# Four of layer 1's eight modulation groups run between the experts of layer 0 and the norm of layer 1

## The chip, the cores and the metric

The kernel runs on one core of a Trainium2 chip. The metric is the time of the whole program in microseconds (us), as the device counts it; the median of several runs is quoted. The engines are PE (TensorE, matrix products), DVE (VectorE), ACT (ScalarE), POOL (GpSimd) and SP (SyncE, which here only issues DMAs). Each engine takes its instructions in the order in which the compiled program lists them.

## The reference, cut to what matters

Two layers of one trunk run over 256 context tokens and 256 latent tokens, with 1024 channels.

```python
for i in range(DEPTH):                       # DEPTH = 2
    mod = silu_c @ w_mod[i] + b_mod[i]       # (6*D) for the latent tokens
    modc = silu_cc @ w_mod[i] + b_mod[i]     # and for the context
    sh1, sc1, g1, sh2, sc2, g2 = ...         # six slices of D channels each
    h = rmsnorm(x, norm1_g[i]) * (1.0 + sc1) + sh1
    mix, mixc = mixing_sublayer(h, hc, w_in[i], ...)     # S5, SSD, attention
    x = x + g1 * mix
    h2 = rmsnorm(x, norm2_g[i]) * (1.0 + sc2) + sh2
    x = x + g2 * expert_choice_ffn(h2, ...)              # 16 experts
return rmsnorm(x, final_norm_g)
```

The six slices (`sh1`, `sc1`, `g1`, `sh2`, `sc2`, `g2`) are the kinds 0 to 5 of the kernel's modulation. Kinds 0 and 1 are needed by the norm in front of the mixing; kinds 2 to 5 not before the mixing's end.

## The kernel before, in words

`mod_group(l, kind, h)` (L157) computes half of one kind for both token sets. It issues four loads of 512 KB of `w_mod` (`load_w`, L103, on SP's queue) into the tile `w`, and eight small products per load (L165, 32 columns by 128); we call one load with its eight products a unit. The trace lists each product twice, so that a unit has 16 records. After four units ACT copies the result out (L168), PE transposes it (L169) and DVE writes it as `mcol` (L179, L181). A group is thus four units, and four groups are 16.

Groups wait in the list `todo`. `fill(n)` adds n credits and issues a group for every four credits. `win(c0, tiles, evac)` (L543) is the input projection: for each pair of 128-column tiles it takes two loads of `w_in` of 512 KB, calls `fill` unless `c0` is 0, and multiplies with `mm3`. Each such load goes raw into the same tile `w`; ACT rounds it to `wh` (L110), DVE or POOL subtracts to `wl` (L113), and PE multiplies with both (L122 and L125). The tile `w` has three buffers (`NW`), taken in turn by everything that loads into it: w_in, w_mod, and in the expert stage pieces of w_e_up and w_e_down. A load can be issued when the third load before it has been consumed.

At the start of layer 1's mixing two things follow on the experts' last `combine` (L1366 to L1370): the norm (`rs_tok`, L509 to L515) writes `xna` and `xnb`, and `xsave` puts the residual aside in DRAM (L517). Then `norm_rows` transposes them (L244, 8 row blocks), ACT scales and shifts them into `hrow` (L247), and DVE and POOL split them into `hh` and `hl`. `win(0, ...)` multiplies these with the first four w_in loads, and the small time-step projection (L747) follows. The later projections (`win(1024)` and `win(1536)` with a convolution behind them on DVE, then `win(512)`, `win(2576)`, `win(2064)`) run while DVE, POOL, ACT and PE also carry the S5 blocks (L610 to L723) and the SSD scan (L834 to L899).

The text of the kernel does not fix the order of an engine's instructions alone. The framework's scheduler lists them by its own timeline, so that instructions written later can stand earlier; SP's loads of one tile keep their order.

Of the kernel before, what the change touches and what calls it, by code (L numbers as in the profile page):

```python
# [34 lines left out]
DEPTH, D, T, N = 2, 1024, 512, 256  # L35
# [26 lines left out]
def r(ap):  # L62
    return ap.bitcast(F32R)
# [3 lines left out]
def tile_trunk(ctx: ExitStack, tc: tile.TileContext, a, out, dbg=None, stop=None):  # L67
# [14 lines left out]
    def bank(tag="ps"):  # L82
        return psm.tile([128, 512], F32, name="bk_" + tag, tag=tag, bufs={"mm": 3, "ps": 4, "s5": 1}[tag])
# [58 lines left out]
    todo = []  # L142
# [42 lines left out]
    def fill(n=1):  # L185
        credit[0] += n
        while todo and credit[0] >= 4:
            credit[0] -= 4
            mod_group(*todo.pop(0))
        if not todo:  # L190
            credit[0] = 0
# [49 lines left out]
    def transposed(xn, tts, k, sc, sh, pool, tag, bufs, btag="ps"):  # L241
        ps = bank(btag)
        for tt in tts:
            PE.transpose(ps[:, tt * 128:tt * 128 + 128], xn[tt][:, k * 128:k * 128 + 128], ident)  # L244
        h = pool.tile([128, 512], F32, name="hrow", tag=tag, bufs=bufs)
        for st in sorted({tt // 2 for tt in tts}):
            S.activation(h[:, st * 256:st * 256 + 256], ps[:, st * 256:st * 256 + 256], AF.Identity,  # L247
                         bias=sh[:, k, st:st + 1], scale=sc[:, k, st:st + 1])
        return h
# [213 lines left out]
    def mixing(l, mods):  # L463
        full = l == 0
# [56 lines left out]
        def norm_rows(ks):  # L521
            for k in ks:
                if full:
                    for kind in range(2):
                        mod_unit(0, kind, k, mw[k][kind])
                h = transposed(xn, [0, 1, 2, 3], k, mods["sc1"], mods["sh1"], bp, "t2", T2,
                               ("mm" if k % 2 else "s5") if full else "ps")
                V.tensor_copy(r(hh[:, k, :]), h)
                (G if k % 2 and not full else V).tensor_tensor(r(hl[:, k, :]), h, hh[:, k, :], op=OP.subtract)

        def hv(k, t0, t1):
            return r(hh[:, k, t0:t1]), r(hl[:, k, t0:t1])

        def wcols(wh, wl):
            return tuple(lambda m, k, v=v: v[:, k, m * 128:m * 128 + 128] for v in (wh, wl))
# [22 lines left out]
        if full:  # L558
            ub = [bank() for _ in range(4)]
            for kh in range(2):  # L560
                norm_rows(range(4 * kh, 4 * kh + 4))
                wu = []
                for i in range(0, 4, 2):
                    wu.append(load_w(a["w_in"][l], 4 * kh, 4, 128 * i, 256))
                if kh == 0:
                    for k in range(5, 8):
                        mod_load(k)
                for i in range(0, 4, 2):
                    wh, wl = wu[i // 2]
                    mm3(ub[i:i + 2], wcols(wh, wl), [lambda m, k=k: hv(4 * kh + k, 0, 512) for k in range(4)], kh == 0, kh == 1)  # L570
            for m in range(4):
                ev_u(m, ub[m])
        else:
            norm_rows(range(8))
            win(0, [0] * 4, ev_u)
        dump("hh%d" % l, hh)
        todo.extend((l, kind, h) for kind in range(2, 6) for h in range(2))
        if l + 1 < DEPTH:
            todo.extend((l + 1, kind, h) for kind in range(2) for h in range(2))
        sp = s5_params(l, slab) if full else X["sp"]  # L580
        c_lo = 0 if full else 32
        nl = 64 - c_lo
# [241 lines left out]
        for d in range(2):  # L824
# [4 lines left out]
            for ix, c in enumerate(seq):  # L829
# [17 lines left out]
                if need:  # L847
# [7 lines left out]
                    for g in range(2):  # L855
                        Rf = []
                        for p_ in range(2):
                            R = bp.tile([128, 4, 128], F32, name="R", tag="R", bufs=RB)
                            for q in range(4):
                                h = d * 8 + 4 * g + q  # L860
# [16 lines left out]
                        for q in range(4):  # L877
                            h = 4 * g + q
# [685 lines left out]
```

## Time and profile before

| | |
|---|---|
| runs | 2170.76, 2180.32, 2176.95 us; median 2176.95 |
| profiled execution | span 2175.6 us from the first to the last instruction; its time outside the span is not listed |
| PE, DVE, ACT, POOL busy | 86%, 48%, 26%, 27% |
| mean granted TensorE clock | 0.933 of full |
| stages | mixing of layer 0 to about 660 us, experts of layer 0 to 1214, mixing of layer 1 to about 1660, experts of layer 1 to the end |

A stage is read by its own rows: how long each engine was busy in it, the granted clock (PEclk, 1.00 is 2.4 GHz and 0.50 is 1.2 GHz) and what the DMA engines moved. A busy PE in such a row counts the tail of a pipelined product, so that a stretch of spaced products looks fuller than it is.

### The profile page before, as it was taken

The numbers are of one execution on the slowest core, as the hardware profiler recorded it, in microseconds if no ns is written. First come the engines' busy times: TensorE is split into PE (matmuls) and PEld (weight loads), VectorE is DVE, ScalarE is ACT, GpSimd is POOL, SyncE is SP. The second block draws the span as 40 slices with busy tenths as digits, with TensorE's granted clock in tenths as the row PEclk, the third lists the DMA queues.
The fourth block names the chain that finished last, engine by engine and source line by source line (L and its number), as shares of the span: only waits on it lengthen the run. The fifth ranks groups of instructions, "written<-read, shape, count | busy, mean of one in ns | idle before, by whom it ended". The sixth has DMA issues, their size and how long they took to land. (4 is left out here: it accounts for less than half of the span.)

```text
span 2175.6 us, 29618 instructions
## 1 busy us (share of the span) xinstructions
PE 1879.4 (86%) x11292; PEld 1127.1 (52%) x11292; DVE 1040.2 (48%) x2234; ACT 554.9 (26%) x1200; POOL 589.0 (27%) x644
## 2 busy tenths in 40 slices
PE   6899999999999997986897898989998997776675
PEld 4577777788787432322332576778897322111111
DVE  6888786663256227121123469788656222212122
ACT  4335644442343100000000433535443100000000
POOL 1645476542242002000003235486533000000000
PEclk9999989999998998998898998989998899999798
DMA  9464333336345998999999355343477899999997
GB/s 268 156 183 127 114 90 107 99 104 220 90 155 203 410 349 351 409 408 409 404 409 351 107 185 172 107 129 86 125 244 271 348 409 409 409 409 409 409 409 274
DMA packets 265310, 561.72 MB, mean 258 GB/s; under 512 B 44048, under 2 KB 132560, under 8 KB 264912
## 3 DMA queue, kind: packets, MB, share of 16 engines
q1 hardware_dynamic: 232864, 541.83, 68.0%
q10 hardware_dynamic: 32304, 18.00, 3.0%
q8 instruction: 89, 1.46, 0.3%
q14 instruction: 53, 0.43, 0.1%
HBM read 552.00 MB, written 7.77 MB: 257 GB/s over the span
## 5 line engine op out<-in xcount | busy, mean ns | idle before, releaser
L122 PE MATMUL bk_mm<-hh,wh 128*128 128x512 f32 (+1 forms) x704 | 254.2, 375 | 12.5 <-ACT xp L800 6.7
L122 PE MATMUL bk_mm<-hl,wh 128*128 128x512 f32 (+1 forms) x704 | 247.6, 365 | 0.0
L113 POOL TENSOR_TENSOR wl<-w,wh 128x1024 fp32r<-128x1024 f32 x64 | 157.0, 2452 | 223.5 <-ACT wh L110 171.1
L110 ACT ACTIVATE wh<-w 128x1024 fp32r<-128x1024 f32 x140 | 147.9, 1058 | 215.9 <-PE bk_mm L122 106.6
L125 PE MATMUL bk_mm<-hh,wl 128*128 128x512 f32 (+1 forms) x704 | 163.0, 361 | 1.5 <-POOL wl L113 1.5
L122 PEld LDWEIGHTS bk_mm<-hh,wh 128*128 128x128 f32 x704 | 139.6, 199 | 36.1 <-ACT xp L800 8.2
L122 PEld LDWEIGHTS bk_mm<-hl,wh 128*128 128x128 f32 x704 | 139.6, 199 | 17.7 <-issue 1.4
L113 DVE TENSOR_TENSOR wl<-w,wh 128x1024 fp32r<-128x1024 f32 x76 | 99.8, 1315 | 72.6 <-ACT wh L110 32.4
L125 PEld LDWEIGHTS bk_mm<-hh,wl 128*128 128x128 f32 x704 | 119.6, 195 | 20.0 <-POOL wl L113 1.7
L1389 PE MATMUL bk_mm<-rb,xeT 128*64 128x512 f32 x512 | 122.1, 601 | 3.3 <-DMA rb<-w_e_up 2.0
L1419 PE MATMUL bk_mm<-xw,xeT 128*32 128x512 f32 x448 | 107.3, 628 | 16.5 <-DMA xw<-w_e_gate 11.4
L1424 DVE SCALAR_TENSOR_TENSOR hd<-fth,bk_mm 64x512 f32<-64x512 f32 x16 | 10.9, 681 | 208.4 <-ACT fth L1422 208.4
L1441 DVE SCALAR_TENSOR_TENSOR YE<-bk_mm,grow 32x512 f32<-32x512 f32 x64 | 44.0, 687 | 129.6 <-PE bk_mm L1436 115.8
L1422 ACT ACTIVATE fth<-bk_mm 64x512 f32<-64x512 f32 x16 | 9.4, 590 | 377.7 <-PE bk_mm L1419 377.7
L1389 PE MATMUL bk_mm<-xw,xeT 128*64 128x512 f32 x320 | 82.1, 613 | 13.5 <-DMA xw<-w_e_gate 13.5
L603 POOL MEMSET rb<- 128x256 f32 x2 | 1.2, 588 | 319.0 <-PE bk_mm L1389 305.0
L1393 DVE SCALAR_TENSOR_TENSOR fth<-fth,bk_mm 128x512 f32<-128x512 f32 x16 | 11.0, 687 | 157.3 <-ACT fth L1392 157.3
L1389 PEld LDWEIGHTS bk_mm<-rb,xeT 128*64 128x64 f32 x512 | 40.1, 139 | 78.6 <-issue 69.8
L1409 DVE SCALAR_TENSOR_TENSOR YE<-bk_mm,grow 32x512 f32<-32x512 f32 x64 | 44.0, 687 | 73.3 <-PE bk_mm L1405 56.5
L1419 PE MATMUL bk_mm<-rb,xeT 128*32 128x512 f32 x304 | 68.0, 603 | 8.3 <-DMA rb<-w_e_up 6.1
L1366 PE MATMUL bk_ps<-YE,Gt 128*128 128x512 f32 x128 | 61.7, 612 | 11.9 <-DVE YE L1441 9.1
L1419 PEld LDWEIGHTS bk_mm<-xw,xeT 128*32 128x32 f32 x448 | 24.1, 114 | 88.7 <-issue 55.5
(560 smaller groups left out, 3883.5 us busy)
## 6 DMA issues: line engine op xcount, KB each, us to landing
xw<-w_e_gate SPq DMA_DIRECT2D x67, 1024.0 KB, 11.5
rb<-w_e_up SPq DMA_DIRECT2D x59, 1024.0 KB, 17.4
xw<-w_e_down SPq DMA_DIRECT2D x54, 1024.0 KB, 14.0
w<-w_in SPq DMA_DIRECT2D x92, 512.0 KB, 4.7
rb<-w_e_gate SPq DMA_DIRECT2D x43, 1024.0 KB, 16.6
w<-w_mod SPq DMA_DIRECT2D x80, 512.0 KB, 4.1
xw<-w_e_up SPq DMA_DIRECT2D x29, 1024.0 KB, 14.0
w<-w_e_down SPq DMA_DIRECT2D x46, 512.0 KB, 14.0
```

The costliest lines, as they stand in the source:

```text
L110: S.activation(r(hi), raw, AF.Copy)
L113: e.tensor_tensor(r(lo), raw, hi, op=OP.subtract)
L122: PE.matmul(ps, wh(m, k), xv, start=first and k == 0 and i == 0, stop=False)
L125: PE.matmul(ps, wl(m, k), xs[k](m)[0], start=False, stop=last and k == n - 1)
L1366: PE.matmul(ps, Gt[:, tt - tts[0], e // ne, :], YE[:, tt // 2 if full else 0, n, :], start=True, stop=True)
L1389: PE.matmul(ps[64 * n:64 * n + 64, :], xeT[:, k, e, :], w[:, n * 512:n * 512 + 512], start=k == 0, stop=k == 7)
L1393: V.scalar_tensor_tensor(th, th, 1.0, pg, op0=OP.add, op1=OP.mult)
L1409: V.scalar_tensor_tensor(YE[q0:q0 + 32, si, n, :], py[o:o + 32, :], 0.5, g2[o:o + 32, si, n * 512:n * 512 + 512], op0=OP.mult, op1=OP.mult)
L1419: PE.matmul(pg[o:o + 32, :], xeT[:, k, e, :], w[:, n * 512:n * 512 + 512], start=k == 0, stop=k == 7)
L1422: S.activation(th[:64], pg[:64], AF.Tanh, scale=0.5)
L1424: V.scalar_tensor_tensor(hd[64:128], th[:64], 1.0, pg[:64], op0=OP.add, op1=OP.mult)
L1441: V.scalar_tensor_tensor(YE[q0:q0 + 32, 0, n, :], py[o:o + 32, :], 0.5, g2[o:o + 32, 1, n * 512:n * 512 + 512], op0=OP.mult, op1=OP.mult)
```

## The change

Before, all eight groups of kinds 2 to 5 of layer 1 enter the list after `win(0)`, and `fill` draws them out among the projections. Now, for layer 1, they enter the list in front of the norm's transposes, and `fill(16)` issues four of them there: kinds 2 and 3. The other four (kinds 4 and 5) stay in the list and are drawn by the same calls as before. Layer 0 is untouched. Lines behind the edit move down by two.

```diff
         else:
+            todo.extend((l, kind, h) for kind in range(2, 6) for h in range(2))
+            fill(16)
             norm_rows(range(8))
             win(0, [0] * 4, ev_u)
         dump("hh%d" % l, hh)
-        todo.extend((l, kind, h) for kind in range(2, 6) for h in range(2))
-        if l + 1 < DEPTH:
-            todo.extend((l + 1, kind, h) for kind in range(2) for h in range(2))
+        if full:
+            todo.extend((0, kind, h) for kind in range(2, 6) for h in range(2))
+            todo.extend((1, kind, h) for kind in range(2) for h in range(2))
```

What the scheduler makes of it shows on SP first. The next rows are SP's loads before, from the last pieces of expert 15 (w_e_up, w_e_down) on.

```order
L1345 DMA w<-w_e_up 128x1024
L1345 DMA w<-w_e_down 128x2x512 x2
L1345 DMA wh<-w_e_down 128x2x512
L1345 DMA wl<-w_e_down 128x2x512
L106 DMA w<-w_in 128x4x256 x4
L742 DMA w<-w_in 128x8x16
L517 DMA xsave<-x 128x2x1024
L106 DMA w<-w_in 128x4x256
L106 DMA w<-w_mod 128x2x512 x4
L106 DMA w<-w_in 128x4x256 x2
```

These are the same loads on SP now.

```order
L1347 DMA wl<-w_e_down 128x2x512
L106 DMA w<-w_mod 128x2x512 x6
L517 DMA xsave<-x 128x2x1024
L106 DMA w<-w_mod 128x2x512 x10
L106 DMA w<-w_in 128x4x256 x4
L744 DMA w<-w_in 128x8x16
L106 DMA w<-w_in 128x4x256
L106 DMA w<-w_mod 128x2x512 x4
L106 DMA w<-w_in 128x4x256 x2
```

All 16 loads of the four groups now stand ahead of the four w_in loads of `win(0)`. Behind them two w_in and four w_mod loads alternate as before, until the last group; after it 13 w_in loads follow in a row.

On PE, these rows stood between expert 15's last products (L1405), the last `combine` (L1366) and `win(0)` before.

```order
L1405 MATMUL bk_mm<-wl,hT 64x512 x2
L1366 MATMUL bk_ps<-YE,Gt 128x512 x4
L244 MATMUL bk_ps<-kc,xna 128x128 x8
L244 MATMUL bk_ps<-kc,xnb 128x128 x8
L244 MATMUL bk_ps<-kc,xna 128x128 x2
L244 MATMUL bk_ps<-kc,xnb 128x128 x2
L122 MATMUL bk_mm<-hh,wh 128x512 x2
L244 MATMUL bk_ps<-kc,xna 128x128 x2
L244 MATMUL bk_ps<-kc,xnb 128x128 x2
L122 MATMUL bk_mm<-hl,wh 128x512 x2
```

On PE now, from the end of the last `combine` (L1368 here) to the first product of `win(0)`, these rows stand (units 8 and 9, pairs of L244 and an L169 are left out between the two pieces).

```order
L1368 MATMUL bk_ps<-YE,Gt 128x512 x4
L165 MATMUL bk_mm<-w,sil 32x128 x24
L169 MATMUL bk_mm<-kc,cpart 128x128
L165 MATMUL bk_mm<-w,sil 32x128 x8
L244 MATMUL bk_ps<-kc,xna 128x128 x8
L244 MATMUL bk_ps<-kc,xnb 128x128 x8
L165 MATMUL bk_mm<-w,sil 32x128 x8
```

```order
L165 MATMUL bk_mm<-w,sil 32x128 x24
L169 MATMUL bk_mm<-kc,cpart 128x128
L165 MATMUL bk_mm<-w,sil 32x128 x32
L169 MATMUL bk_mm<-kc,cpart 128x128
L122 MATMUL bk_mm<-hh,wh 128x512
```

Fourteen of the 16 units (x8 is one) stand behind the last `combine`, and no product of `win(0)` stands ahead of the last of them. The other two stand earlier: one in an S5 block beside expert 15, one behind expert 15's last products. From L747 on, PE's order is the same as before through 16 units of the later groups.

Then, in the SSD scan (L850 to L882), PE had these rows before.

```order
L715 MATMUL bk_s_9981<-rb_9574,rb_9573 128x32 x2
L165 MATMUL bk_mm<-w,sil 32x128 x2
L850 MATMUL bk_ps<-BC 128x128
L165 MATMUL bk_mm<-w,sil 32x128 x19
L880 MATMUL bk_ps<-wt,xdt 64x128
L882 MATMUL bk_ps<-e_9743,H 64x128
```

And now it has these there.

```order
L715 MATMUL bk_s_10165<-rb_9757,rb_9756 128x32
L717 MATMUL bk_s_10165<-rb_9758,rb_9757 128x32 x2
L852 MATMUL bk_ps<-BC 128x128
L882 MATMUL bk_ps<-wt,xdt 64x128
L884 MATMUL bk_ps<-e_9927,H 64x128
```

From the second half of the convolution to the attention's start, the 16 units that stood among the other work are gone, and projections of the later `win` calls stand earlier than they did.

## Rows read from the trace of the kernel before

**Rows 1.** The page: span, then busy share and instructions of PE.
```profile
span 2175.6 us, 29618 instructions
PE 1879.4 (86%) x11292; PEld 1127.1 (52%) x11292; DVE 1040.2 (48%) x2234; ACT 554.9 (26%) x1200; POOL 589.0 (27%) x644
```

**Rows 2.** Windows over the transition and layer 1's mixing: stretch, length, busy time per engine.
```profile
core 0: us, PE busy (x) PEld busy (x) DVE busy (x) ACT busy (x) POOL busy (x), PEclk, DMA share, GB/s
1185.00:1214.00 29.00, 26.24 (x80) 9.74 (x76) 17.43 (x25) 8.97 (x22) 10.78 (x11) 0.92 0.44 130
1214.00:1223.00 9.00, 4.25 (x19) 3.88 (x20) 5.60 (x32) 5.46 (x12) 0.14 (x2) 0.66 0.30 117
1223.00:1247.00 24.00, 24.00 (x115) 19.50 (x115) 9.31 (x12) 10.81 (x19) 10.06 (x6) 0.98 0.24 72
...
1271.00:1323.00 52.00, 46.13 (x349) 37.54 (x350) 47.31 (x77) 14.46 (x26) 23.24 (x30) 0.87 0.55 170
1323.00:1370.00 47.00, 37.34 (x359) 29.47 (x359) 40.28 (x83) 22.61 (x65) 22.12 (x28) 0.86 0.51 157
1370.00:1426.00 56.00, 55.36 (x520) 43.06 (x518) 41.13 (x89) 23.69 (x61) 32.51 (x37) 0.99 0.41 116
...
1450.00:1550.00 100.00, 92.33 (x750) 80.46 (x749) 79.12 (x190) 47.32 (x115) 61.62 (x65) 0.92 0.33 93
```

**Rows 3.** Timeline of PE there: start, length, instruction, [idle before <- releaser].
```profile
1207.53 1.88 PE L1405 MATMUL bk_mm<-wl,hT 128*64 128x512 f32 x4
1210.28 3.67 PE L1366 MATMUL bk_ps<-YE,Gt 128*128 128x512 f32 x8 [0.88 <-DVE YE L1409]
1218.28 1.94 PE L244 MATMUL bk_ps<-kc,xna 128*128 128x128 f32 x8 [4.33 <-DVE rs_u L216]
...
1223.17 1.00 PE L122 MATMUL bk_mm<-hh,wh 128*128 128x512 f32 x2
...
1224.23 0.38 PE L244 MATMUL bk_ps<-kc,xnb 128*128 128x128 f32 x2
...
1246.96 1.07 PE L747 MATMUL bk_mm<-hh,w 128*32 128x512 f32 x8
```

**Rows 4.** Timeline of SP: when runs of loads were issued, over how long.
```profile
1185.94 20.43 SPq L106 DMA_DIRECT2D w<-w_in  x4
...
1214.71 0.37 SPq L517 DMA_DIRECT2D xsave<-x  x1
1235.47 0.37 SPq L106 DMA_DIRECT2D w<-w_in  x1
1239.32 12.23 SPq L106 DMA_DIRECT2D w<-w_mod  x4
```

**Rows 5.** Timeline of ACT: the first two roundings of layer 1's w_in.
```profile
1190.84 1.06 ACT L110 ACTIVATE wh<-w 128x1024 fp32r<-128x1024 f32 x1 [1.39 <-DMA w<-w_in]
1207.73 1.06 ACT L110 ACTIVATE wh<-w 128x1024 fp32r<-128x1024 f32 x1 [4.13 <-PE bk_mm L1405]
```

**Rows 6.** The tile w_mod, layer 1's 32 loads: time from issue to landing.
```profile
DMA to landing us min/median/max: 3.6/4.2/5.7
```

**Rows 7.** Timeline of PE: two units in a row, and one that waited for its load.
```profile
1250.42 1.06 PE L165 MATMUL bk_mm<-w,sil 128*32 128x128 f32 x32
...
1330.29 0.65 PE L165 MATMUL bk_mm<-w,sil 128*32 128x128 f32 x16 [1.31 <-DMA w<-w_mod]
```

**Rows 8.** Windows: the four microseconds ahead of win(0).
```profile
1219.00:1223.10 4.10, 3.63 (x17) 3.23 (x16) 1.07 (x3) 2.55 (x5) 0.14 (x2) 0.50 0.00 0
```

**Rows 9.** Windows of line L165 alone (PE, PEld, clock, DMA): the last 16 units.
```profile
1323.00:1370.00 47.00, 7.33 (x128) 4.62 (x128) 0.86 0.51 157
1370.00:1426.00 56.00, 7.95 (x128) 3.92 (x128) 0.99 0.41 116
```

**Rows 10.** Timeline of PE: waits for DVE in the SSD scan and after it.
```profile
1344.11 1.22 PE L865 MATMUL bk_ps<-R,slr 128*128 128x512 f32 x2 [2.35 <-DVE H L899]
...
1435.58 0.39 PE L122 MATMUL bk_mm<-hh,wh 128*128 128x256 f32 x1 [1.22 <-DVE mcol L181]
```

## The prediction

> **What bounds the kernel now.** I read the page first: PE is the engine with the most work, 86% of the span of 2175.6 us [rows 1]. That is an average, so I went to the windows over the place that the change touches [rows 2]. The reader should see four different stretches there. Up to 1214 the experts of layer 0 end. From 1214 to 1223 nearly everything is idle: PE has 4.25 us of work in 9 us, the clock has dropped to 0.66 on average and the DMA engines move little. Here the norm of layer 1 is a chain: the timeline of PE shows the last `combine` ending at 1210.28 + 3.67 = 1213.95, a wait of 4.33 us for the norm's root on DVE, and the first product of `win(0)` at 1223.17 [rows 3]. From 1223 to 1247 PE is full (24.00 of 24.00 us) and DVE idles: `win(0)` takes 1246.96 - 1223.17 = 23.8 us, and its end releases everything that follows, the S5 blocks (through `us`) and the convolution. From 1271 to 1323 DVE is the fuller engine (47.31 of 52 us, 91%), and PE follows it. From 1323 on both are near full: PE 37.34 of 47 us, then 55.36 of 56 us, and 92.33 of the 100 us from 1450.
>
> The last view is SP's queue. Before, `win(0)` never waits for weights: its four loads were issued from 1185.94 on, as the buffers of `w` came free from expert 15 [rows 4], and ACT had rounded two of them by 1208.8, before the norm began [rows 5]. Those are the loads that now stand behind 16 others.
>
> **The change, part by part.** (a) *What 16 units cost at the transition, in PE time.* Two units in a row take 1.06 us, one alone 0.65 us [rows 7], so 16 take 8 to 10 us. PE has 4.75 idle microseconds from 1214 to 1223 [rows 2], so some of that is free. That is the smaller half.
>
> (b) *Their loads.* This sets the end. The tile `w` has three buffers: load n waits until unit n-3 has run on PE. A load lands 4.2 us after its issue (3.6 to 5.7) [rows 6], and a unit takes about 0.6 us, so three units go through in one round of 4.8 us, not 1.8. I follow the queue with the times of before. Load 1 takes the buffer that went to w_in at 1185.94; unit 1 runs beside an S5 block. Unit 2 follows on L1405, which ended at 1209.4 [rows 3]; loads 2 to 4 have landed by then, and load 5 is issued at about 1210. Units 3, 4 and 5 run behind the `combine`, at 1214.0 to 1215.7. Load 6, issued behind unit 3 at 1214.7, lands at 1218.9, and unit 6 runs to 1219.5. The first transposes (L244) stand behind it in PE's order and start at 1219.5, not at 1218.28: 1.2 us late. Load 7 stands behind `xsave` on SP, which waits for the residual until 1214.7 [rows 4]; it lands by about 1221 and is covered by the transposes. Unit 8 stands behind the transposes of the sixth row block, which ended at 1224.6 [rows 3] and now end near 1225.3; it ends at 1225.9. From there nothing covers the loads: unit 11 ends one round later, at 1230.7, unit 14 at 1235.5, and only then is the buffer free for the first w_in load. That lands at 1239.7, ACT takes 1.06 us to round it [rows 5], and `win(0)` starts at 1240.8 instead of 1223.2: **17.6 us late**. The 16th unit is through by about 1238.4 and does not hold it. Later w_in loads follow within a few microseconds and are hidden behind the first one's products.
>
> `win(0)` itself I leave at 23.8 us. It then has all rows of `hh` and `hl` ready, but it starts on a slow clock, as before (0.50 from 1219 to 1223.1) [rows 8]. So its end, and with it S5 and the convolution, comes about 17.5 us later. Bounds from the landing: three rounds and a load at the fastest landing, 3.6 us, give 4 x 0.6 = 2.4 us less, and with unit 8 not held by the transposes some 2 us less again, 13 us; at 5.7 us they give 6 us more, 23.5 us.
>
> The Trainium skill's page "DMA: Bandwidth & Descriptors", Rules for kernel authors, says to issue a DMA early, compute, and wait late, so that its fixed cost overlaps; it speaks against this order, which takes an early issue away from w_in. By the page's fit (2.0 us fixed, in its section Anatomy of one DMA) a 512 KB load would take 3.2 us, an estimate; the landing in the trace is a microsecond longer, and by the page the delay would be some 4 us smaller.
>
> (c) *xsave, ACT, DVE and POOL.* `xsave` keeps its place against the residual; its megabyte now shares the DMA with loads 6 to 8, inside the landing's spread. The four copies L168 and the `mcol` writes stand among idle stretches of ACT and DVE (5.46 and 5.60 of 9 us) [rows 2]. Nothing is charged. Without that cover they would cost under 1 us each.
>
> (d) *What the projections get back.* From L747 on, PE's order is unchanged through 16 units, up to about 1323 in the times of before. Over this stretch DVE leads (91%), and nothing is given back; the delay passes through. Behind it 16 units are gone. Their busy time is 7.33 + 7.95 = 15.3 us [rows 9], which counts the tails of short pieces; at 0.5 us a unit it is 8.2 us. Two waits go with them: 1.31 us for a load [rows 7] and 1.22 us of a projection for `mcol` [rows 10]. That gives 10.7 to 17.8 us at most. Not all of it comes back: in front of some pieces' successors PE waits for DVE anyway, 2.35 us at 1344.11 [rows 10], and from 1323 to 1370 PE has 9.7 idle microseconds as it is, with DVE at 86% [rows 2]. From 1370 to 1426 PE is full, and there 7.95 us of units are real time; afterwards the projections that were pulled forward shorten a PE that is over 90% full. I take **11.5 us**, with 5 and 17 as ends.
>
> *Sum.* +17.5 - 11.5 = +6 us. The experts of layer 1 start when the mixing ends and stream their weights from then, so the shift passes to the end. The profiled span of 2175.6 becomes 2181.6; the median of the runs is 1.35 us above that span, so the time is **2183 us**.
>
> **The rivals.** *Nothing is given back (slower).* The place is the SSD scan and S5 after 1323. Its point of decision is whether DVE (86%, then 73%) [rows 2] or its chain with ACT lets PE use the freed time. For it: from 1271 to 1370 DVE is fuller than PE, and the S5 blocks' start moves with `win(0)`. Against it: PE is full from 1370 to 1426. The return would be 5 us or less, and the time 2177 + 12.5 to 13 = 2190 us.
>
> *It evens out.* The delay is at its lower end, 13 us, and the return at 13 or more: 2177 us or a little less. For it: each round's landing near 3.6 us is within the rows.
>
> *The units gate the rest (faster).* Before, each pair of w_in loads stands behind four w_mod loads, and those wait for PE. With the later groups gone, 13 w_in loads follow each other, and the scan could close PE's 9.7 idle microseconds as well: a return of 17 + 8 = 25 us against 13, 2165 us. Against it: those idle times are waits for DVE.
>
> *The clock.* Before the first product of `win(0)` PE would run single units between waits from 1214 to 1241, and the clock stood at 0.50 after far less idleness [rows 8]. It is in the forecast as a start no faster than before; if it stayed low over the units too, each round would grow by half a microsecond, 1.5 us in all, inside the range. The Trainium skill, "TensorE: Matmul & The Clock Gate", HAM oscillation, describes short bursts of products between DMA waits that fall back to the low clock each time. The trace agrees for the 4.1 us in front of `win(0)`; no row here shows a longer run of bursts.
>
> That the change does not do what it says is excluded by the listed order: 16 units do stand at the transition.
>
> **How the numbers follow.** The forecast (a delay of about 17, most of the PE time given back) has 0.62. Nothing given back: 0.23. Evens out: 0.08. Faster: 0.07. About 0.5% (10.9 us) is what a measurement of this kernel can tell from no change. The forecast and the even case lie within it, 0.70; slower takes 0.23, faster 0.07. The range reaches from 2172 (even case and a little more) to 2192, which takes in most of the slower case.
>
> **What would show it.** In the profile after: the first product of `win(0)` near 1241 and L747 near 1264; one round of three units about 4.8 us apart between 1225 and 1238, PE waiting for DMA in front of them; a clock near 0.5 there; the conv stretch as long as before; and the stretch that answered to 1323 to 1426 shorter by some 8 us. The prediction is wrong if `win(0)` starts before 1235 (then the loads pipeline better than one round per landing), or if the stretch from L747 to the experts of layer 1 is not 5 us shorter than before.

## The result, and the profile after

The changed kernel takes 2196.65 us (median), the kernel before 2173.86 us in the same comparison: ratio 1.0097, 95% interval 1.0072 to 1.0122. It is slower by about 21 us; 2183 was forecast, with 2172 to 2192 as the range, and the measured time lies above it. The page of the profiled execution has a span of 2193.9 us, 18.3 more than before [rows 1], and PE with 3.0 us more busy time:

```profile
span 2193.9 us, 29598 instructions
PE 1882.4 (86%) x11292; PEld 1133.9 (52%) x11292; DVE 1039.8 (47%) x2234; ACT 556.2 (25%) x1200; POOL 589.1 (27%) x644
```

The transition, first on SP (start, length of the run of loads, instruction; before: [rows 4]):

```profile
1184.36 28.01 SPq L106 DMA_DIRECT2D w<-w_mod  x6
1212.47 0.42 SPq L517 DMA_DIRECT2D xsave<-x  x1
1212.98 21.07 SPq L106 DMA_DIRECT2D w<-w_mod  x10
1235.63 8.84 SPq L106 DMA_DIRECT2D w<-w_in  x4
```

The first w_in load left at 1235.63 instead of 1185.94. On PE the units stand as follows (timeline; before: [rows 3]):

```profile
1207.70 3.67 PE L1368 MATMUL bk_ps<-YE,Gt 128*128 128x512 f32 x8 [0.30 <-DVE YE L1411]
1211.30 1.52 PE L165 MATMUL bk_mm<-w,sil 128*32 128x128 f32 x48
...
1216.54 1.08 PE L165 MATMUL bk_mm<-w,sil 128*32 128x128 f32 x16 [2.99 <-DMA w<-w_mod]
...
1228.70 0.73 PE L165 MATMUL bk_mm<-w,sil 128*32 128x128 f32 x16 [2.04 <-DMA w<-w_mod]
1230.65 1.08 PE L165 MATMUL bk_mm<-w,sil 128*32 128x128 f32 x16 [1.22 <-DMA w<-w_mod]
...
1236.70 1.08 PE L165 MATMUL bk_mm<-w,sil 128*32 128x128 f32 x16 [1.14 <-DMA w<-w_mod]
1238.31 1.08 PE L165 MATMUL bk_mm<-w,sil 128*32 128x128 f32 x16 [0.53 <-DMA w<-w_mod]
...
1241.68 0.79 PE L122 MATMUL bk_mm<-hh,wh 128*128 128x512 f32 x1 [1.41 <-ACT wh L110]
...
1265.76 1.06 PE L749 MATMUL bk_mm<-hh,w 128*32 128x512 f32 x8
```

The reader sees single units, most of them with a wait for DMA in front, and `win(0)` at 1241.68, which waits for ACT to round the first w_in. The forecast had 1240.8 for that and about 1264 for the time-step projection (L749 here, L747 before); it came at 1265.76. The last six units start 9.61 us apart from first to last, 1.92 us each, so a round of three took 5.8 us, not 4.8.

So the delay was there. What was not there is the return. The next rows are windows (stretch, length, busy time and records of PE, PEld, DVE, ACT and POOL, granted clock, share of the DMA engines, GB/s) between landmarks of the mixing: from the time-step projection to the end of the BC convolution, to the end of the SSD scan, to the transpose of `dgr` (L973 before), to the last attention scores, to the end of attention, to the gated output of S5, to the first expert. First the kernel before, then the changed one.

```profile
1247.00:1346.60 99.60, 86.49 (x770) 67.56 (x770) 77.61 (x144) 30.62 (x67) 39.76 (x50) 0.91 0.59 184
1346.60:1415.30 68.70, 64.59 (x561) 50.31 (x561) 51.79 (x103) 35.85 (x98) 31.50 (x33) 0.92 0.40 116
1415.30:1459.90 44.60, 36.23 (x353) 31.89 (x349) 38.68 (x76) 17.80 (x37) 37.14 (x37) 0.96 0.48 138
1459.90:1536.90 77.00, 75.53 (x598) 64.54 (x598) 62.69 (x150) 38.28 (x92) 45.33 (x50) 0.94 0.33 93
1536.90:1563.00 26.10, 22.44 (x150) 21.98 (x150) 14.00 (x36) 9.08 (x19) 18.84 (x20) 0.80 0.34 78
...
sum 439.80, PE 395.71 PEld 338.67 DVE 318.36 ACT 179.24 POOL 216.99; mean PE 56.53 PEld 48.38 DVE 45.48 ACT 25.61 POOL 31.00
```

```profile
1265.80:1362.50 96.70, 82.84 (x718) 65.83 (x717) 77.42 (x144) 32.79 (x71) 39.27 (x50) 0.95 0.56 173
1362.50:1436.00 73.50, 64.12 (x522) 53.11 (x522) 60.77 (x120) 38.71 (x102) 40.22 (x41) 0.95 0.25 69
1436.00:1471.30 35.30, 23.53 (x175) 22.12 (x175) 29.80 (x59) 11.65 (x27) 30.06 (x32) 0.76 0.28 79
1471.30:1552.50 81.20, 80.01 (x589) 68.34 (x589) 60.84 (x144) 37.69 (x90) 42.59 (x49) 0.85 0.27 75
1552.50:1578.10 25.60, 23.44 (x145) 22.85 (x145) 15.54 (x35) 9.32 (x20) 17.12 (x20) 0.73 0.39 95
...
sum 438.40, PE 385.67 PEld 335.96 DVE 319.37 ACT 178.65 POOL 215.29; mean PE 55.10 PEld 47.99 DVE 45.62 ACT 25.52 POOL 30.76
```

PE is busy for 10.0 us less, with 16 units gone, and the whole is only 1.4 us shorter: PE's idle time grew from 44.1 to 52.7 us. Up to `dgr` 7.4 us had been won (212.9 to 205.5). The fourth window, with no unit in it before or after, then loses 4.2: about the same products (598 and 589 records) take 80.0 us instead of 75.5, at a granted clock of 0.85 instead of 0.94. In windows of 8 us from `dgr` on, the changed kernel has:

```profile
1464.00:1472.00 8.00, 2.75 (x35) 2.56 (x35) 6.92 (x26) 0.00 (x0) 3.23 (x4) 0.54 0.34 92
1472.00:1480.00 8.00, 6.81 (x18) 3.17 (x17) 8.00 (x22) 2.43 (x8) 4.93 (x9) 0.50 0.09 23
1480.00:1488.00 8.00, 8.00 (x52) 8.00 (x51) 3.80 (x10) 3.69 (x10) 4.10 (x7) 0.68 0.01 2
1488.00:1496.00 8.00, 8.00 (x34) 6.25 (x34) 6.26 (x13) 1.18 (x3) 5.40 (x7) 0.53 0.29 66
1496.00:1504.00 8.00, 8.00 (x60) 8.00 (x60) 5.45 (x12) 4.65 (x9) 0.17 (x1) 0.83 0.06 10
1504.00:1512.00 8.00, 8.00 (x72) 6.66 (x71) 4.26 (x8) 5.55 (x17) 3.96 (x2) 1.00 0.62 190
```

and the kernel before:

```profile
1452.60:1460.60 8.00, 4.01 (x62) 3.31 (x61) 7.65 (x24) 2.82 (x9) 4.63 (x3) 0.92 0.32 92
1460.60:1468.60 8.00, 7.18 (x23) 4.43 (x22) 5.76 (x16) 2.45 (x7) 5.68 (x7) 0.50 0.28 89
1468.60:1476.60 8.00, 8.00 (x64) 7.50 (x63) 6.89 (x21) 4.42 (x12) 4.94 (x11) 0.94 0.01 2
```

In both kernels the clock falls to 1.2 GHz (0.50) where PE has waited around `dgr`. Before, it is back within 16 us; in the changed kernel it rises once, falls again to 0.53 and is full only from 1504 on.

### The profile page after: what moved, and what is told of

Read it like the earlier page. It is cut to its first block, busy times and chain, and to the rows that moved or that the text cites. A ratio compares the mean times of both kernels' runs of the same rounds, so it can differ in the third digit from the quotient of the medians.

```text
span 2193.9 us, 29598 instructions
## 1 busy us (share of the span) xinstructions
PE 1882.4 (86%) x11292; PEld 1133.9 (52%) x11292; DVE 1039.8 (47%) x2234; ACT 556.2 (25%) x1200; POOL 589.1 (27%) x644
## 4 chain that ended last, share of the span: by engine, by line
PE 55%; DMA 23%; DVE 13%; POOL 3%; issue 2%; ACT 2%; SPq 1%; DVEq 0%; ACTq 0%; POOLq 0%
PE bk_mm L122 12%; PE bk_mm L1391 7%; PE bk_mm L125 6%; PE bk_mm L1421 4%; PE bk_mm L1407 3%; DMA wl<-w_e_up 3%; DMA wh<-w_e_up 3%; PE bk_ps L1285 3%; DMA rb<-w_e_up 2%; DMA xw<-w_e_gate 2%; DMA w<-w_e_up 2%; PE bk_mm L1438 2%; DMA w<-w_e_down 2%; DMA w<-w_e_gate 2%; PE bk_ps L1039 2%
## 5 line engine op out<-in xcount | busy, mean ns | idle before, releaser
L122 PEld LDWEIGHTS bk_mm<-hl,wh 128*128 128x128 f32 x704 | 140.9, 200 | 17.5 <-issue 1.0
L1426 DVE SCALAR_TENSOR_TENSOR hd<-fth,bk_mm 64x512 f32<-64x512 f32 x16 | 10.9, 681 | 208.9 <-ACT fth L1424 208.9
L165 PE MATMUL bk_mm<-w,sil 128*32 128x128 f32 x1280 | 60.1, 298 | 15.8 <-DMA w<-w_mod 13.8
```

What stands on the lines that cost most here:

```text
L122: PE.matmul(ps, wh(m, k), xv, start=first and k == 0 and i == 0, stop=False)
L165: PE.matmul(ps[32 * j:32 * j + 32, :128], sil[:, 2 * u + i, :], w[:, i, j * 128:j * 128 + 128], start=u == 0 and i == 0, stop=u == 3 and i ...
```

## The experiments

Each kernel's profile gives two lengths, beside the time of the whole. The **transition** runs from the start of the `combine`'s last product to the start of the time-step projection, 33.6 us before. The **rest** runs from there to the start of the last expert's last product, 914.0 us before. The table shows both as differences to the kernel before. Each is from one execution: the expert stage of layer 1 alone takes up to 2.5 us more than in the kernel before, and the `combine`, which both lengths leave out, comes between 6.9 us earlier and 6.5 us later than there (5.1 later in before_aheadlist, whose list is the kernel before's up to it). So the two lengths need not add up to the whole, and a difference of a few microseconds in one of them says little by itself. The changed kernel has +21.4 and -0.6; its `combine` came 2.6 us earlier, and that makes 18.2 of the 18.3 us.

| kernel | whole, ratio (95%) | transition | rest | order behind the time-step projection |
|---|---|---|---|---|
| after | 1.0097 (1.0072 to 1.0122) | +21.4 | -0.6 | its own |
| drop4 | 0.9961 (0.9942 to 0.9979) | -0.1 | -10.0 | its own |
| extra4 | 1.0151 (1.0128 to 1.0174) | +20.8 | +12.6 | its own |
| one | 1.0043 (1.0023 to 1.0063) | +3.3 | +7.6 | its own |
| two | 1.0009 (0.9997 to 1.0022) | +3.9 | -0.4 | its own |
| after_droplist | 1.0136 (1.0095 to 1.0177) | +34.2 | -9.6 | drop4's |
| drop_afterlist | 1.0039 (1.0018 to 1.0060) | +7.4 | -0.6 | after's |
| extra_beforelist | 1.0157 (1.0117 to 1.0197) | +33.8 | -5.9 | before's |
| before_extralist | 1.0102 (1.0067 to 1.0137) | +7.7 | +9.6 | extra4's |
| after_droplist2 | 1.0061 (1.0044 to 1.0079) | +21.5 | -7.9 | drop4's |
| before_extralist2 | 1.0071 (1.0049 to 1.0092) | +0.1 | +9.4 | extra4's |
| ahead | 1.0012 (0.9994 to 1.0031) | +16.5 | -20.3 | its own |
| ahead_droplist | 1.0051 (1.0031 to 1.0071) | +16.9 | -10.6 | drop4's |
| after_beforelist | 1.0104 (1.0084 to 1.0125) | +21.4 | -3.8 | before's, units left out |
| after_aheadlist | 1.0028 (1.0013 to 1.0043) | +21.7 | -14.6 | ahead's |
| before_aheadlist | 1.0100 (1.0080 to 1.0121) | +0.0 | +19.4 | ahead's, units put in |
| drop_beforelist | 1.0024 (1.0008 to 1.0039) | -0.1 | +0.3 | before's, units left out |
| behind_aheadlist | 1.0023 (1.0005 to 1.0041) | +17.1 | -20.5 | ahead's |
| behind | 1.0089 (1.0070 to 1.0108) | +17.1 | -1.0 | its own |

**The two halves apart, and smaller doses.** drop4 has only the return: the four groups are left out and constants stand in their place. extra4 has only the delay; one and two move one and two groups instead of four.

```diff
 # drop4, against the changed kernel
-            todo.extend((l, kind, h) for kind in range(2, 6) for h in range(2))
-            fill(16)
+            for kind in (2, 3):
+                mods[names[kind]] = const.tile([128, 8, 2], F32, name="mcol1_%d" % kind)
+                G.memset(mods[names[kind]], 0.5)
+            todo.extend((l, kind, h) for kind in range(4, 6) for h in range(2))
 # extra4, against the kernel before; mod_group writes duplicates with a tag into tiles of their own
+            for kind in (2, 3):
+                for h in range(2):
+                    mod_group(1, kind, h, "x")
             norm_rows(range(8))
 # one and two, against the changed kernel
-            fill(16)
+            fill(4)        # two: fill(8)
```

> The kernel before, with the first four of layer 1's modulation groups (kinds 2 and 3) left out altogether and their tiles filled with 0.5 instead; nothing is added at the transition. It measures alone what the projections give back when 16 units go. The theory of the prediction (PE time that is removed in the mixing mostly comes back, 11.5 us): about 2162 to 2165 us, 0.5% under the kernel before. The rival (the mixing of layer 1 is led by DVE and by chains, the units lie in PE's gaps): within 4 us of the kernel before.

> The kernel before, with all eight groups left among the projections and four more groups (the same products, into tiles that nobody reads) at the transition. It measures alone what the transition costs. The theory of the prediction (17.5 us there, and a return of 11.5 us that this kernel doesn't have): about 2191 us. The rival (20 us or more at the transition and no return worth the name): the same time as the changed kernel, 2194 to 2197 us, since taking the groups out of the projections is worth nothing.

> One group at the transition instead of four, seven among the projections. The first w_in load now waits for unit 2 alone, which ran at 1206.8, so win(0) should start near 1223 as in the kernel before. The theory of the prediction: no delay and a quarter of the return, 3 us under the kernel before. The rival: no delay and no return, the same time as before within 2 us.

> Two groups at the transition. The first w_in load waits for unit 6, which ran at 1217.6 in the changed kernel, so it lands near 1222 and win(0) starts near 1223 to 1225. Both theories: a delay of 0 to 3 us; with a return of 5 to 6 us (the prediction's) 2 to 6 us under the kernel before, without a return 0 to 3 us over it. If the cost went by units and not by rounds of landings behind unit 8, half of the 20 us would show: 10 us over.

As whole times, drop4 (2168.9 us) lies between its two forecasts, two (1.0009) agrees with no return, and extra4 (2208.8) and one (2187.0) are slower than either theory had them. The transitions bear out the rounds of landings: one and two pay 3.3 and 3.9 us for 4 and 8 units (none and 0 to 3 expected), the changed kernel 21.4 for 16, so the delay does not go by the number of units.

The rests do not add up. drop4 gives back 10.0 us in the rest, the changed kernel, with the same code behind the norm, 0.6. extra4 has exactly the kernel before's work in the rest and loses 12.6 there; one loses 7.6. So something moved the rest by some ten microseconds either way that is neither the work removed nor the delay. The lists of the built programs named a suspect: behind L747 drop4 and the changed kernel have the same instructions on every engine, but in another order, from the SSD scan on. That the edit at the transition shifts the timeline by which the scheduler lists is the likely reason; no run shows it apart. My forecast had looked at the order only up to the removed units.

**The order, crossed.** For these, the order that the scheduler gave one kernel was recorded and pinned in another, engine by engine, with edges that fix the place in the list and add no wait.

```diff
+    for i in tc.nc.cur_bb.bb.instructions[tc_mark[-1]:]:
+            lanes.setdefault(str(i.engine), []).append(i)
...
+        own = [lane[k] for k in tab[1:n + 1]]
+        for p, q in zip(own, own[1:]):
+            tc.add_manual_dep(q, p.name, dep, reason="list")
```

> The changed kernel; behind the norm of layer 1 each engine's instructions are pinned to the list that the kernel drop4 had there (the two have the same instructions behind the norm, so nothing is added or removed, only their order on each engine). In the profiles so far the stretch from the time-step projection to the end was 10.0 us shorter than the kernel before's in drop4 and 0.6 us shorter in the changed kernel. Theory that the list eats the return: the changed kernel loses about 9.4 us of its 2196.65, to some 2187, 1.0055 of the kernel before, with the transition as it was (about 21 us late against the last combine). Rival, that the later arrival itself eats it (loads, waits or the granted clock as that kernel meets them): no change, 2196 to 2197, about 1.010.

> The cross of the run above: drop4 (16 units fewer, none at the transition; four groups of layer 1 are not computed, so two modulation columns are constants) with the changed kernel's list behind the norm. Theory of the list: it loses about 9.4 us of what drop4 gained, 2168.9 to some 2178, about 1.002 of the kernel before. Rival, the later arrival: as drop4, about 2169, 0.996, since nothing arrives late here.

> extra4 (the kernel before plus four duplicate groups at the transition) with the kernel before's list behind the norm, where both have the same instructions. extra4 took 33 us more than the kernel before, of which its profile had 20.8 at the transition and 12.6 behind the time-step projection. Theory of the list: the 12.6 go, 2208.8 to some 2196, about 1.0095. Rival, the later arrival: they stay, about 2209, 1.015.

> The cross of the run above: the kernel before, no work added, with extra4's list behind the norm. Theory of the list: some 12.6 us slower than the kernel before, about 2188, 1.006. Rival, the later arrival: as the kernel before, 2175, 1.000.

As whole times all four came out slower than the theory of the order had them. For drop_afterlist its 1.002 lies inside the interval; the other three are misses, extra_beforelist close to its rival. The mark stood at the norm, and a foreign order of the norm and of the rounding of `win(0)`'s weights cost another 7 to 13 us in the transition. In the rest, however, three of them took what the order takes, not what the kernel takes: -9.6 where drop4 had -10.0, -0.6 where the changed kernel had -0.6, +9.6 where extra4 had +12.6. The fourth, extra_beforelist, has -5.9 where the kernel before's order gives 0 and extra4's own +12.6. The mark was therefore moved to the time-step projection.

> The changed kernel with drop4's list, pinned only from the time-step projection (L747 of the kernel before) on, so that the transition keeps the changed kernel's own list. In the four crossed runs before, whose pinning began at the norm, the projections of win(0) came later in all of them than their own lists had them (8.7 us later in the kernel before), but the stretch from the time-step projection to the last expert went with the list: drop4's list -10.0 in drop4 and -9.6 in the changed kernel, the changed kernel's list -0.6 in itself and -0.6 in drop4, extra4's list +12.6 in itself and +9.6 in the kernel before; the kernel before's list 0 in itself and -5.9 in extra4. Theory of the list: the changed kernel loses some 9 us of its 2196.65, to about 2187, 1.0055, with that stretch -9 to -10 and the transition +21 as it was. Rival, the later arrival: no change, 2196 to 2197, 1.010, the stretch at -0.6.

> The kernel before, nothing added or removed, with extra4's list from the time-step projection on; its own list up to there. Theory of the list: the transition as in the kernel before, the stretch behind it 9 to 13 us longer, together 2184 to 2188, 1.0045 to 1.006. Rival, that a late arrival eats the time: nothing arrives late here, so 2175, 1.000.

Both confirm it in the whole time. The changed kernel with drop4's order takes 2190.3 instead of 2196.65 (2187 expected); the kernel before, with nothing added and nothing late, takes 2191.8 instead of 2176.1 when it runs in extra4's order (2184 to 2188 expected). A late start cannot do that. Nor is it the pinning that costs: drop4's order takes -10.0 in drop4, where nothing is pinned, and -9.6, -7.9 and -10.6 where it is (after_droplist, after_droplist2, ahead_droplist). In the profile of before_extralist2 the windows from the end of the SSD scan to the last scores answer to rows three and four of the kernel before above:

```profile
1413.10:1470.80 57.70, 41.63 (x374) 36.64 (x375) 41.69 (x86) 19.25 (x43) 40.97 (x41) 0.80 0.42 121
1470.80:1554.10 83.30, 80.87 (x590) 69.75 (x589) 63.54 (x141) 38.98 (x91) 44.18 (x52) 0.85 0.26 75
```

The first of the two is 13.1 us longer, with 16.1 us of PE idle instead of 8.4, the second 6.3 us longer at the lower clock. Both carry nearly the records that they had (374 and 353, 590 and 598). What PE waits for longest there, between the end of the BC convolution and `dgr`, is a DMA of the S5 blocks, a wait that the kernel before does not have in that stretch (line, releaser, us, times, longest):

```profile
PE bk_s L833 <- DMA rb<-kd: 6.5, 2, 4.6
```

**What the units cost with the order held.** This is the term that I had to forecast, measured by itself: the kernel before's order, the 16 units left out of it.

> The changed kernel with the kernel before's list from the time-step projection on, the four groups that it no longer has there left out of the list and every other instruction in the kernel before's order: the units are taken from the projections without a new order. The prediction gave this return 11.5 us (5 to 17). If the units bounded the work there, the stretch from the time-step projection to the last expert is 10 to 11.5 us shorter than in the kernel before, 2196.65 less 10 gives 2186, 1.005. If they lay in time that PE waits through anyway, or kept TensorE's clock up there, the stretch is 0 to 4 us shorter, 2193 to 2197, 1.0085 to 1.010.

> drop4 (16 units fewer, none at the transition; two modulation columns are constants) with the kernel before's list from the time-step projection on, the missing units left out of it. In the run after_beforelist the stretch from the time-step projection to the last expert was 3.8 us shorter than in the kernel before, where drop4 with its own list had 10.0. If what taking the units away gives back is a matter of the list, it is 2 to 5 us shorter here too: 2175 less 4, some 2171, 0.998. If it is the early start that gives drop4 its 10 us, the stretch is 10 shorter here as well, 2165, 0.9955.

after_beforelist has -3.8 and 2196.5 us as a whole, inside the forecast for a small return. drop_beforelist has +0.3, and as a whole it is no faster than the kernel before (1.0024) although 16 units are gone; both of its forecasts were faster. These are the second and third window of drop_beforelist (the scan, and up to `dgr`):

```profile
1344.20:1411.80 67.60, 59.32 (x415) 47.38 (x417) 49.17 (x99) 35.30 (x96) 27.22 (x32) 0.82 0.21 56
1411.80:1458.90 47.10, 38.91 (x291) 36.41 (x286) 39.35 (x75) 17.75 (x36) 38.22 (x39) 0.78 0.31 89
```

With 208 records fewer than before (706 instead of 914) the two take 114.7 us instead of 113.3. PE idles 16.5 us there instead of 12.5, and what is left runs at 0.82 and 0.78 instead of 0.92 and 0.96. (after_beforelist has 112.1 us, at 0.83 and 0.85.) PE's longest waits in this stretch of drop_beforelist are the first of the next rows; under them stand three of the kernel before (line, releaser, us, times, longest):

```profile
PE bk_s L836 <- DVE rb L827: 4.8, 2, 3.1
PE bk_ps L972 <- DVE BC L938: 3.1, 1, 3.1
PE bk_ps L1002 <- DVE wt L991: 2.9, 1, 2.9
PE bk_s L769 <- ACT rb L764: 2.8, 1, 2.8
PE bk_ps L1095 <- DVE dgr L1094: 2.6, 1, 2.6
```

```profile
PE bk_s L648 <- ACT rb L643: 2.7, 1, 2.7
PE bk_ps L973 <- DVE dgr L972: 2.6, 1, 2.6
PE bk_ps L880 <- DVE wt L869: 0.8, 1, 0.8
```

ACT's `rb` and `dgr` were waited for before as well. The wait for `BC` and the one for DVE's `rb` (L836 here, L715 in the kernel before) are new, and the one for `wt` grew from 0.8 to 2.9 us: these are products in front of which units stood in the kernel before's list. S5 blocks and the scan hand results to and fro between DVE, ACT and PE. In this order the units filled gaps in that exchange, and the clock stood higher with them; taken away, they leave the gaps.

**The transition.** ahead gives the 16 loads buffers of their own, eight of them issued ahead of `xsave`, so that w_in keeps its three. behind also puts the products between the halves of `win(0)` and after it.

```diff
 # ahead, against the changed kernel: m8("mw") is a free tile of the layer's pool
+            for t_ in todo[:2]:
+                mod_ahead(*t_, m8)          # before xsave
...
+            fill(8)
+            for t_ in todo[:2]:
+                mod_ahead(*t_, m8)
+            fill(8)
-            fill(16)
 # behind, against ahead
+                with tc.issue_after(last):  # the last product of a half of win(0)
+                    fill(8)
```

> The changed kernel with the loads of its 16 units in buffers of their own (four free tiles of the layer's pool, two units each), the first eight issued ahead of the write of xsave, so that the three buffers of the projections keep the first w_in blocks, as in the kernel before. Theory that the rounds of landings through three buffers make the delay of win(0): from the last combine to the time-step projection 8 to 14 us longer than in the kernel before, in place of 21.4, since 10 us of products remain and 8 MB must land. Rival, that the products themselves make it (their clock, their place in PE's order): about 21 as before. What lies behind is the scheduler's new list and isn't known better than -10 to +10 by the lists seen so far: 2176 to 2196 in all, 1.0005 to 1.010.

> The kernel ahead with drop4's list from the time-step projection on. If both theories hold, the transition costs 8 to 14 us and the stretch behind gives back 10: 2171 to 2180, 0.998 to 1.002, a tie with the kernel before or a small gain. If the products make the delay, 2185, 1.005; if the list does nothing, as the kernel ahead.

> The changed kernel with the list of the kernel ahead from the time-step projection on (the same instructions behind it; in ahead that stretch was 20.3 us shorter than in the kernel before, in the changed kernel 0.6). Theory of the list alone: -20 here too, 2196.65 less 19.7 gives 2177, 1.0005, with the transition 21 us longer than in the kernel before as it was. Rival, that ahead's gain came with its buffers or its loads: the stretch at -0.6 to -10 as with the other lists, 2187 to 2197.

> The kernel before, all its work, with the list of the kernel ahead from the time-step projection on for the instructions that both have; the last four groups (and ScalarE's instructions up to the last of them) are left to the scheduler. ahead's stretch behind the time-step projection was 20.3 us shorter with 16 units fewer. If those 16 units cost their 10 us of products under this list, the stretch is about 10 us shorter than in the kernel before and the whole 2166, 0.995, faster than both kernels. If they lie in time that PE waits through, about 20 shorter, 2156, 0.991. If the list is worth nothing once the units stand in it, 2175, 1.000.

> The kernel ahead (16 units at the transition, their loads in buffers of their own), with the units no longer ahead of win(0) on TensorE: the first eight between its two halves, the other eight behind it, when their loads have landed; and ahead's list from the time-step projection on. The units then cost their products, about 10.4 us (16 of 0.65), in place of the 16.5 that ahead's transition took more than the kernel before's. With the list as in ahead and after_aheadlist (14.6 and 20.3 us shorter behind the time-step projection): 2175 + 10.4 less 14.6 to 20.3 is 2165 to 2171, 0.9955 to 0.998, faster than both kernels. If landings still hold TensorE there, 16 us stay and the whole ties, 2171 to 2177.

> The kernel above with the scheduler's own list behind the time-step projection. The transition as above, 10.4 us longer than in the kernel before; behind it the lists of these same instructions have given -0.6 to -20.3 so far: 2165 to 2185, 0.9955 to 1.0045.

The size of the transition was a miss in the four that move the loads: 16.5 to 17.1 us instead of 8 to 14 (ahead, ahead_droplist), or of 10.4 with the units behind `win(0)` (behind_aheadlist, behind). In behind_aheadlist the rows say why (POOL's timeline, PE's, then windows):

```profile
1231.00 0.10 POOL L944 MEMSET xp<- 128x4 f32 x1 [18.71 <-DMA xsave<-x]
...
1231.09 2.51 POOL L660 TENSOR_TENSOR hl<-hrow,hh 128x512 fp32r<-128x512 f32 x2
```

```profile
1232.41 0.80 PE L239 MATMUL bk_mm<-hl,wh 128*128 128x512 f32 x1 [5.97 <-POOL hl L660]
...
1244.56 3.25 PE L293 MATMUL bk_mm<-mw,sil 128*32 128x128 f32 x106
...
1260.05 3.05 PE L293 MATMUL bk_mm<-mw,sil 128*32 128x128 f32 x104
```

```profile
1230.00:1235.00 5.00, 2.59 (x6) 2.11 (x7) 1.48 (x3) 2.61 (x6) 2.60 (x4) 0.58 0.93 345
1235.00:1240.00 5.00, 5.00 (x18) 3.96 (x18) 2.37 (x3) 2.20 (x4) 3.27 (x3) 0.74 0.02 6
```

`win(0)` began on time here (1223.1), but then PE waited 5.97 us for POOL's half of `hl`: a clearing of `xp`, listed ahead of it on POOL, ran only when `xsave` had landed. `xsave` was issued at 1218.2 behind eight loads of 512 KB, with four more behind it from 1226.3 on, and landed at 1231.0. Of the 17.1 us the units take 8.1 (1244.56 to 1248.78 and 1260.05 to 1263.97), at full clock. The other 9 are this wait and what came after it: `win(0)` then runs at 0.58 and 0.74, where the kernel before had 0.98 over all of it [rows 2], and 9 less 5.97 leaves some 3 us for that, an estimate. In ahead the same clearing waited until 1231.38. Issuing `xsave` first was not run.

The order did the rest. ahead's own order is the best seen, 20.3 us shorter than the kernel before's rest, 20.5 in behind_aheadlist and 14.6 in the changed kernel, which falls from 2196.65 to 2180.4 by it (2177 expected). ahead in drop4's order falls back to drop4's rest, -10.6, and to 2188.2 as a whole (2171 to 2180 expected). ahead and behind differ only at the transition, by 0.6 us, and by 19 us in the rest: 2176.5 against 2191.5 us (for behind 2165 to 2185 was expected). It is not an order that carries over to other work: put into the kernel before, with the 16 units and ACT's instructions up to the last of them placed by the scheduler among it, it costs 19.4 us, where all three forecasts had a gain or a tie. That is 39.7 us over ahead's rest, 34 of them up to the end of the scan, where the units were put in. No version that does all the work beats the kernel before; ahead and two tie with it (1.0012, 0.9994 to 1.0031, and 1.0009, 0.9997 to 1.0022).

## Why the prediction was wrong, step by step

**(b), the delay: right in its mechanism, 3.9 us too small.** The first w_in load was issued at 1235.63; the prediction's queue had 1235.5, two rounds after unit 8. `win(0)` started 0.9 us later than forecast, the time-step projection within 2 us. That these times agree so well is in part luck: the `combine` came 2.6 us earlier in this execution. Against it the delay is 21.4 us, not 17.5, though inside the bounds of 13 to 23.5. The rounds were longer than forecast, 5.8 us, with landings of 3.6, 4.4 and 7.6 us (min, median, max) against [rows 6]. Issue early and wait late, the rule of the Trainium skill's page "DMA: Bandwidth & Descriptors" (Rules for kernel authors), holds here: the w_in loads that were issued 49.7 us later came too late for `win(0)`. The fit by which I had the delay some 4 us smaller stands on that page of the Trainium skill (Anatomy of one DMA) for DMAs that GpSimd issues, and these loads are on SP's queue; the measured landings decide.

**(a) and the clock: half right.** Fifteen units on PE from 1206.76 on sum to 12.4 us, over the 8 to 10 that I had, because seven of them ran at 1.08 us, where the granted clock was 0.67 (1222.0 to 1241.7), between its two levels of 1.2 and 2.4 GHz. I had priced this rival at 1.5 us in all; a round was 1.0 us longer than 4.8. The Trainium skill, "TensorE: Matmul & The Clock Gate" (HAM oscillation), describes such bursts between DMA waits that fall back to the low clock; this trace agrees, with those seven units. The 4.1 us of [rows 8], in which I had seen agreement, are transposes behind a wait for DVE and not such bursts.

**(c), nothing charged: right for this kernel.** `xsave` landed 6.8 us after its issue, at 1219.3; POOL waited for it, but the first `hl` was not due before 1223.25. In behind the same step would have been wrong by 9 us. The rows were misread here all the same: 5.46 and 5.60 of 9 us [rows 2] are the busy times of ACT and DVE, not their idle ones (3.54 and 3.40), so the prediction's "nearly everything is idle" does not hold there. No term of the sum hangs on that.

**(d), the return: wrong, and this is the step that failed.** The term is 11.5 us; the changed kernel's rest is 0.6 us shorter. Of the 12.3 us by which the span missed its forecast (18.3 instead of 6) that is 10.9; the delay adds 3.9, and the early `combine` takes off 2.6. I took 11.5 of 15.3 us of busy time [rows 9], on the ground that PE is full from 1370 to 1426 (55.36 of 56 us [rows 2]) and that "there 7.95 us of units are real time". Two things were missing.

First, a full PE does not bound a stretch if part of what fills it is filling. With the kernel before's order held, taking out the 16 units is worth between -0.3 and 3.8 us, not 11.5. The rows that speak for it were on the table: waits of PE for DVE right among the units [rows 10], DVE at 86% next door [rows 2]. The rival that nothing is given back rested on them, and I gave it 0.23; it priced the delay at the same size and the return at up to 5 us, and had 2190, which is still 6 us short: it took the delay as 17.5 too.

Second, I took the order behind L747 as given. I read that it was unchanged "through 16 units" and argued from the old rows behind them. The scheduler had listed the same instructions anew from the SSD scan on, and that alone moves the rest: -20.3, -10.0 and -0.6 for the very same instructions (ahead, drop4 and after). Inside one kernel, the changed one, ahead's order is worth 14.0 us of the rest and some 16 of the whole time. The changed kernel got one of the poorer ones. In drop4's it takes 2190 us, in ahead's 2180.

The sum is thus +21.4 of delay, a return of 0.6 us in the order that the changed kernel got, and a `combine` that came early.

**The signs I had named.** `win(0)` near 1241, L747 near 1264, waits for DMA in front of the units, a low clock: all seen; the rounds were 5.8 us apart, not 4.8. "The stretch from L747 to the experts of layer 1 is not 5 us shorter" was the sign for a wrong prediction, and it is 1.4 us shorter. The stretch that answers to 1323 to 1426 did become shorter, by 4.5 us from the end of the BC convolution to `dgr` (113.3 to 108.8), and by 7.4 with the stretch in front of it; part of what was won there was lost behind it, where I had expected a gain.

**What stays open.** The runs show that the order moves the time and through which waits and clock, but not which feature of an order makes it good: the profile shows it only afterwards. Within one order the rest still differs by up to 6 us between kernels (-5.9, -3.8 and +0.3 with the kernel before's), which these single profiles don't explain. Nor is it shown that the units cost nothing in other orders. Among the scheduler's own, the two kernels with all 16 units in the rest have 0 and +12.6 (before, extra4), the four without them -0.6 to -20.3 (after, behind, drop4, ahead): fewer instructions may help the scheduler to a better order. Six draws do not decide that.

## What to carry to other kernels

Work that stands beside a wait can be free, and then moving it away gives back nothing in that order: before counting busy time as a gain, look whether the instructions next to it wait for another engine, and what the clock will do when the gap is bare. Where a scheduler lists the program, an edit in one place re-lists what follows; compare the order of the whole remainder, take a change of some tenths of a per cent as possibly one draw of that order (here the orders span 14 to 20 us, 0.6 to 0.9%), and pin the order when one part of a change is to be measured by itself. A load that is put ahead in a queue delays every load behind it and whoever waits for its buffer; name them all. Here POOL's clearing of a tile was one of them.

## What the runs showed that I had not expected

- The same instructions, in two orders that both come from the scheduler, differ by 20 us over a stretch of 914 (ahead and the changed kernel), and by 14 us where only the order was exchanged (after_aheadlist). PE's busy time up to the first expert is 372.2 us in ahead and 385.7 in the changed kernel, in part since the clock stands lower there (0.95 and 0.85 from `dgr` to the last scores), and its idle time 47.5 and 52.7.
- 16 units more at the transition (extra4) cost 33 us, 16 units fewer behind it (drop4) gain 8.5. Of the 33 us, 12.6 lie behind the transition, where no work was added: they are the order's.
- With eight loads of 512 KB ahead of it in the queue and four behind, a write of 1 MB landed 12.8 us after its issue (1218.2 to 1231.0), where it had taken 6.8 in the changed kernel.
